# A two-layer streaming-encoder trunk: value passes by token halves at the boundary into the attention, and a reordered first projection

## The chip, the cores and the metric

One core of one Trainium2 chip runs the whole program. The metric is the device time of one execution in microseconds, the median of the runs shown; lower is better. Engines are named as the profile does: PE (TensorE matmul), PEld (its weight loads), DVE (VectorE), ACT (ScalarE), POOL (GpSimd), SP (SyncE, which here issues every DMA).

## The reference

One sequence of 512 tokens with 1024 features passes through two layers. Cut to what matters:

```python
c_act = jax.nn.silu(c)
for i in range(2):
    sh1, sc1, g1, sh2, sc2, g2 = jnp.split(c_act @ w_ada[i] + b_ada[i], 6, axis=-1)
    u = x * (1.0 + sc1) + sh1
    y = gla_mixer(u, ...) if i == 0 else chunk_attention(u, ...)   # both: u @ w_in, mix, @ w_out
    x = layer_norm(ALPHA * x + (1.0 + g1) * y, ln_g[i, 0], ln_b[i, 0])
    u = x * (1.0 + sc2) + sh2
    y = squared_relu_mlp(u, ff_w1[i], ff_w2[i])                    # 1024 -> 4096 -> 1024
    x = layer_norm(ALPHA * x + (1.0 + g2) * y, ln_g[i, 1], ln_b[i, 1])
```

`gla_mixer` is a gated linear attention with 4 heads. `chunk_attention` has 16 heads of 64 features, with a learned bias by distance and a softmax over the keys of the token's own and all earlier chunks.

## The kernel before, in words

Features lie on the 128 partitions, tokens on the free axis; the residual x is eight tiles `xs` of 128 x 512. Every large product is made of three matmuls (`mm3`): each operand is split into a high part (rounded to the matmul's type) and a low part (the rest), and high x high, high x low and low x high are summed in one PSUM bank. So every 128 x 1024 piece of a weight is one "unit": a DMA into a `raw` buffer (5 of them), an ACT copy that makes `whi`, a DVE subtraction that makes `wlo` (POOL for a few units). `wp` holds four such pairs. Some weights that later stages need are split early into `fhi`/`flo`: `f` units stay in SBUF, `c` units are written to DRAM and read back later, already split, by `x` units.

All units stand in one list, `plan`. `next_w` takes the next pair, and `fill(n)` emits units until n pairs are ready. The classes around the engines (`InOrder`, line 39) keep DVE, ACT, POOL and PE instructions in the order in which the code emits them.

The stages, in order of time:

- **First projection** (`gla`, line 622). The 48 modulation vectors of a layer are dot products of `csil` = silu(c), spread over the partitions, with rows of `w_ada`: a DMA of 512 KB and one DVE multiply with a running sum for each (`ada_unit`, line 127). For each of the eight feature tiles k: the multiplies for shift and scale of k, then u[k] = x[k] * scale + shift (high part on ACT, a full copy `uf` and the low part on DVE), the weight unit of k, then 24 matmuls of 512 columns into all eight PSUM banks, 8 high x high, 8 high x low, 8 low x high.
- **GLA**, and its output product, which runs into a `boundary`.
- **`boundary`** (line 328): output product, residual, layer norm and the next u, by two halves of 256 tokens. While the second half is normalised (`stats1`, `stats2`, `ap1`, `ap2`), PE runs the next stage's first four weights (`fg`) on the first half, then on the second, 256 columns at a time.
- **MLP**, in four groups; in layer 0 its units are interleaved with the remaining modulation vectors and with 16 `c` units.
- **Attention** (`att`, line 893). At the second boundary `fg` is q and k of head pairs 0 and 1. Then `vpass` makes the values in two passes of 96 matmuls (tokens stationary, weights moving, 512 columns), into which the scores and the first softmax of heads 0 and 1 are hung. Then a loop over p = 0 to 5: q of pair p+2, scores of head 2p+2 (`s_mm`), k of pair p+2, scores of head 2p+3, the product with the values for heads 2p and 2p+1 (`pv`). DVE, ACT and POOL make the softmax meanwhile (`s_a`: bias and maximum, `s_b1`: subtract, `s_b2`: exponential; `evac_qk`: bias and split of q and k; `fin1` to `fin3`: division).
- The third boundary, the second MLP, the last boundary.

Of the kernel before, what the change touches and what calls it, by code (L numbers as in the profile page):

```python
# [59 lines left out]
def trunk(ctx, tc, xT, c, ada, cols, gk1, gk2, w_qk, w_v, w_g, w_go, a_qk, a_v, a_tab,  # L60
# [47 lines left out]
    nc.sync.dma_start(out=csil, in_=c.to_broadcast([P, D]))  # L108
# [3 lines left out]
    for _ in range(5):  # L112
        T.matmul(warm, one[:, 0:P], one, start=True, stop=True)
    A.activation(out=csil, in_=csil, func=AF.Silu)
# [12 lines left out]
    def ada_unit(l, t, k):  # L127
        raw = rawp.tile([P, D], F32, tag="raw", name=nm("raw"))
        nc.sync.dma_start(out=raw, in_=ada[l, t * 8 + k])
        if (l, t, k) == (0, SH1, 0):  # L130
            nc.sync.dma_start(out=col, in_=cols)
            for ll in range(2):
                for ty in (SC1, G1, SC2, G2):
                    b = C_ADA + ll * 48 + ty * 8
                    G.tensor_scalar(out=col[:, b:b + 8], in0=col[:, b:b + 8], scalar1=1.0, scalar2=None, op0=ALU.add)
            G.tensor_scalar(out=bq8, in0=col[:, C_BQ:C_BQ + 8], scalar1=0.125, scalar2=None, op0=ALU.mult)
            G.tensor_scalar(out=nbgk, in0=col[:, C_BGK:C_BGK + 4], scalar1=-1.0, scalar2=None, op0=ALU.mult)
            G.tensor_scalar(out=gn2, in0=col[:, C_GN:C_GN + 8], scalar1=-0.5, scalar2=None, op0=ALU.mult)
        if t == SC1 and l == 0:
            nc.sync.dma_start(out=xs[k], in_=xT[k * P:(k + 1) * P, :])  # L140
# [28 lines left out]
    def emit_unit():  # L169
# [23 lines left out]
        if state["pos"] == 3:  # L193
            for q in range(2):
                nc.sync.dma_start(out=raw[:, q * S:(q + 1) * S], in_=what[:, q * S:(q + 1) * S])
        else:
            nc.sync.dma_start(out=raw, in_=what)
        hi, lo = split_w(kind in "fF")
        if state["pos"] == 3:
            V.tensor_copy(hi[:, 0:S], raw[:, 0:S])  # L200
            later.append(lambda: A.copy(out=hi[:, S:D], in_=raw[:, S:D]))
            later.append(lambda: lo_of(V, lo, raw, hi))
            ready_w.append((hi, lo))
            return
        if kind == "s":
            for q in range(2):
                A.copy(out=hi[:, q * S:(q + 1) * S], in_=raw[:, q * S:(q + 1) * S])
        else:
            A.copy(out=hi, in_=raw)
# [57 lines left out]
    def add_mlp(l, fgs, ad, keep=()):  # L267
# [60 lines left out]
    def boundary(src, l, gt, open_lnt, mk_cols, fg_evac, events=None, final=False):  # L328
# [262 lines left out]
        fa = [bank(), bank()]  # L591
        n = 3 if late else 2
        fg(0, fa, range(n))
        ap1(0, 3)
        ap2(0, 2)
        stats1(1)
        ap2(0, 3)
        stats2(1)
        fg(0, fa, range(n, 8))
        ap1(1, 0)  # L600
        for p in range(1, 4):
            ap1(1, p)
            ap2(1, p - 1)
        ap2(1, 3)
        fb = [bank(), bank()]
        fg(1, fb, range(8))
        for hf, pf in ((0, fa), (1, fb)):
            fill(1 + hf)
            rest = ()
            for i in range(4):  # L610
                nxt = fg_evac(i, pf[i // 2][:, (i % 2) * HT:(i % 2 + 1) * HT], hf * HT, (hf + 1) * HT)
                for g in rest:
                    g()
                rest = nxt
            for g in rest:
                g()
# [5 lines left out]
    def gla():  # L622
# [9 lines left out]

        u = [act_r() for _ in range(KT)]
        pss = [bank() for _ in range(8)]
        gk_t = wp.tile([P, D], F32R, tag="whi", name="gk_w")
# [5 lines left out]
        G.memset(eps_rms, RMS_EPS)  # L641
        for k in range(KT):
            emit_unit()
            emit_unit()
            if k == 0:
                emit_unit()
            A.activation(out=u[k][:, 0, :], in_=xs[k], func=AF.Identity, scale=mod(0, SC1, k), bias=mod(0, SH1, k))
# [245 lines left out]
    def att(u):  # L893
        es = ExitStack()
# [3 lines left out]
        vt = [ac.tile([P, 8, 192], F32, name=f"vt{i}") for i in range(4)]  # L898
        for i in range(4):
            G.memset(vt[i][:, :, 64:128], 1.0)  # L900
# [68 lines left out]
        def pv(h):  # L969
# [4 lines left out]
            for j in range(4):  # L974
                T.matmul(ps[:, j * P:S], vt[j][:, p, c0:c0 + P], s[j], start=(j == 0), stop=(j == 3))
# [30 lines left out]
        def vpass(n, hooks):  # L1006
            pvb = [bank() for _ in range(4)]
            for j in range(4):
                w = next_w()
                for kk in range(2):  # L1010
                    k = 2 * j + kk
                    for i in range(4):
                        mm3(pvb[i], uk(u, k, i * P, (i + 1) * P), wk(w, kk, S), k == 0, k == KT - 1)
                hooks[j]()
            for i in range(4):
                ov = vt[i][:, n * 4:(n + 1) * 4, :].rearrange("p a (b c) -> p a b c", c=64)[:, :, 0:3:2, :]
                iv = pvb[i].rearrange("p (a b c) -> p a b c", b=2, c=64)
                if i % 2:
                    V.tensor_copy(ov, iv)
                else:  # L1020
                    A.copy(out=ov, in_=iv)

        def both(*fs):
# [207 lines left out]
```

## Time and profile before

| | |
|---|---|
| median of 3 runs | 1232.88 us (1232.21 to 1233.76) |
| the profiled execution | 1231.73 us |
| its span, first to last instruction | 1229.5 us |
| mean granted TensorE clock | 0.991 of full |
| DMA | 192.68 MB, mean 157 GB/s |

| engine | busy us | share of the span |
|---|---|---|
| PE | 1181.4 | 96% |
| PEld | 986.9 | 80% |
| DVE | 834.3 | 68% |
| ACT | 542.9 | 44% |
| POOL | 185.4 | 15% |

A busy PE means that a matmul was in flight. A row of the timeline gives the start, the length from the first instruction's start to the last one's end, and in brackets how long the engine stood idle before it and what ended that. Consecutive matmuls overlap, so the pace of PE is read from start to start.

### The profile page before, as it was taken

The numbers are of one execution on the slowest core, as the hardware profiler recorded it, in microseconds if no ns is written. First come the engines' busy times: TensorE is split into PE (matmuls) and PEld (weight loads), VectorE is DVE, ScalarE is ACT, GpSimd is POOL, SyncE is SP. The second block draws the span as 40 slices with busy tenths as digits, with TensorE's granted clock in tenths as the row PEclk, the third lists the DMA queues.
The fourth block names the chain that finished last, engine by engine and source line by source line (L and its number), as shares of the span: only waits on it lengthen the run. The fifth ranks groups of instructions, "written<-read, shape, count | busy, mean of one in ns | idle before, by whom it ended". The sixth has DMA issues, their size and how long they took to land.

```text
span 1229.5 us, 15417 instructions
## 1 busy us (share of the span) xinstructions
PE 1181.4 (96%) x5834; PEld 986.9 (80%) x5834; DVE 834.3 (68%) x1269; ACT 542.9 (44%) x864; POOL 185.4 (15%) x195
## 2 busy tenths in 40 slices
PE   8999999899999999999999999898999999999995
PEld 5678887788888888888888877668888888888885
DVE  6779579787667676667864788889865443443467
ACT  3265566365243243343483565573642322322324
POOL 2000001620000000004631132226200000000035
PEclk9999999999999999999999999999999999999998
DMA  8846634118878888764025431322165332232201
GB/s 310 280 155 209 230 110 140 50 41 282 284 268 316 280 291 310 261 250 154 2 78 180 146 135 71 128 87 69 35 204 156 92 106 93 88 107 97 89 15 69
DMA packets 57274, 192.68 MB, mean 157 GB/s; under 512 B 6448, under 2 KB 10800, under 8 KB 57200
## 3 DMA queue, kind: packets, MB, share of 16 engines
q1 hardware_dynamic: 57200, 191.70, 45.7%
q8 instruction: 46, 0.75, 0.3%
q14 instruction: 28, 0.23, 0.1%
HBM read 172.80 MB, written 18.87 MB: 156 GB/s over the span
## 4 chain that ended last, share of the span: by engine, by line
PE 58%; DVE 20%; issue 9%; ACT 8%; POOL 3%; DMA 0%; ACTq 0%; DVEq 0%; POOLq 0%
PE ps L47 58%; DVE af L47 5%; ACT af L47 3%; DVE x L47 3%; DVE ar L47 3%; DVE raw L47 2%; DVE wlo L47 2%; ACT ar L47 2%; POOL af L47 1%; POOL x L47 1%; ACT whi L47 1%; DVE u L47 1%; DVE d L47 1%; DVE y L47 1%; ACT e L47 1%
## 5 line engine op out<-in xcount | busy, mean ns | idle before, releaser
L47 PE MATMUL ps<-ar,whi 128*128 128x512 f32 (+1 forms) x2816 | 806.0, 374 | 6.1 <-ACT ar L47 3.3
L47 PEld LDWEIGHTS ps<-ar,whi 128*128 128x128 f32 x2816 | 515.1, 190 | 104.8 <-DVE ar L47 5.3
L47 PE MATMUL ps<-ar,wlo 128*128 128x512 f32 (+1 forms) x1408 | 513.6, 371 | 0.2 <-DVE wlo L47 0.2
L47 PEld LDWEIGHTS ps<-ar,wlo 128*128 128x128 f32 x1408 | 267.0, 190 | 45.7 <-DVE wlo L47 0.8
L47 ACT CAST whi<-raw 128x1024 fp32r<-128x1024 f32 (+1 forms) x171 | 171.4, 1011 | 212.6 <-PE ps L47 187.0
L47 DVE TENSOR_TENSOR wlo<-raw,whi 128x1024 fp32r<-128x1024 f32 x160 | 199.9, 1254 | 33.3 <-ACT whi L47 31.2
L47 DVE SCALAR_TENSOR_TENSOR x<-ps,mods,x 128x512 f32<-128x512 f32 (+1 forms) x96 | 63.0, 658 | 126.4 <-PE ps L47 126.4
L47 POOL TENSOR_TENSOR x<-x,af 128x512 f32<-128x512 f32 x14 | 25.5, 1847 | 805.9 <-ACT af L47 805.9
L47 DVE SCALAR_TENSOR_TENSOR raw<-raw,csil 128x1024 f32<-128x1024 f32 x96 | 115.8, 1218 | 5.9 <-DMA raw<-ada 5.9
L47 DVE TENSOR_TENSOR h<-r 128x512 f32<-128x512 f32 (+1 forms) x72 | 49.2, 688 | 84.0 <-ACT r L47 83.1
L47 PE MATMUL ps<-ar,fhi 128*128 128x256 f32 (+1 forms) x448 | 91.9, 302 | 8.5 <-DVE ar L47 7.6
L47 ACT ACTIVATE r<-ps 128x512 f32<-128x512 f32 (+1 forms) x72 | 39.0, 548 | 130.7 <-PE ps L47 130.5
L47 PEld LDWEIGHTS ps<-ar,fhi 128*128 128x128 f32 x448 | 71.9, 191 | 12.6 <-DVE ar L47 9.0
L47 PE MATMUL ps<-whi,ar 128*128 128x512 f32 x256 | 81.0, 391 | 0.4 <-ACT whi L47 0.4
L47 DVE TENSOR_TENSOR ar<-h,ar 128x512 fp32r<-128x512 f32 (+1 forms) x72 | 45.5, 633 | 39.5 <-ACT ar L47 38.4
L47 PE MATMUL ps<-ar,flo 128*128 128x256 f32 (+1 forms) x224 | 66.9, 298 | 0.0
L47 ACT CAST ar<-h 128x512 fp32r<-128x512 f32 (+1 forms) x72 | 41.2, 573 | 51.8 <-DVE h L47 51.8
L47 PEld LDWEIGHTS ps<-whi,ar 128*128 128x128 f32 x256 | 48.1, 188 | 11.2 <-ACT whi L47 1.3
L47 PE MATMUL ps<-wlo,ar 128*128 128x512 f32 x128 | 50.2, 392 | 1.5 <-DVE wlo L47 1.5
L47 POOL PARTITION_ALL_REDUCE mb<-af x16 | 31.2, 1952 | 125.0 <-DVE af L47 106.7
L47 ACT ACTIVATE af<-x 128x256 f32<-128x256 f32 (+1 forms) x48 | 22.7, 486 | 57.4 <-POOL af L47 31.4
L47 PEld LDWEIGHTS ps<-ar,flo 128*128 128x128 f32 x224 | 42.8, 191 | 1.3
(144 smaller groups left out, 1072.3 us busy)
## 6 DMA issues: line engine op xcount, KB each, us to landing
raw<-f SPq DMA_DIRECT2D x128, 512.0 KB, 4.2
raw<-ada SPq DMA_DIRECT2D x96, 512.0 KB, 4.8
raw<-a_qk SPq DMA_DIRECT2D x16, 512.0 KB, 4.7
khi_q<-fhi SPq DMA_DIRECT2D x12, 512.0 KB, 3.0
klo_q<-flo SPq DMA_DIRECT2D x12, 512.0 KB, 4.4
wlo<-klo_q SPq DMA_DIRECT2D x12, 512.0 KB, 4.2
whi<-khi_q SPq DMA_DIRECT2D x12, 512.0 KB, 3.3
raw<-w_v SPq DMA_DIRECT2D x8, 512.0 KB, 4.5
```

Of the source, the lines that this page charges most:

```text
L47: r = f(*a, **k)
```

## The change

Three things, in the order in which they run.

1. **First projection.** `c` is loaded as one row of 4 KB, spread by two one-row matmuls into PSUM, and silu reads it from there, in place of a broadcast DMA of 512 KB. `ada` rows, x and the weights of three steps are loaded ahead (`head_dma`), the `ada` rows into the pool `act`. `uf` moves from DVE to ACT, the copies of the weight stand ahead of u[k] on ACT, and the multiplies for k+1 are issued within step k (`head_ada`). Eight small POOL additions become one on DVE. After the loop, the first value weight is split ahead of the PSUM evacuations (`fill(1)`), and four of these eight go from ACT to DVE.
2. **MLP of layer 0.** Four value weights take the place of q and k of pairs 0 and 1 as `f` units, and 18 `c` units (q and k of pairs 1 to 7, and four of the output) take the place of 16, two in every five units instead of one in three.
3. **Boundary into the attention.** With `vfill`, both value passes run here by halves of tokens: pass 0 on the first half (part of it ahead of the statistics), pass 1 on the first half, pass 0 and pass 1 on the second. The weights of pass 1 are split here, between the steps of the normalisation (`fill(2)`, `fill(4)`). Then q and k of pair 0 are made in full width, and the attention loop starts at p = -1, for q and k of pair 1 and the first softmax steps of heads 0 and 1, without `pv`. The values stand in two sets of tiles (`vts`).

```diff
+    crow = act.tile([P, D], F32, tag="act", name="crow")[0:1, :]
+    nc.sync.dma_start(out=crow, in_=c)
...
+        T.matmul(cps, one[0:1, 0:P], crow[:, q * S:(q + 1) * S], start=True, stop=True)
+        A.activation(out=csil[:, q * S:(q + 1) * S], in_=cps, func=AF.Silu)
...
+    def head_dma(k):
+        raws = []
+        for t in (SH1, SC1):
+            raws.append(act.tile([P, D], F32, tag="act", name=nm("hraw")))
+            nc.sync.dma_start(out=raws[-1], in_=ada[0, t * 8 + k])
+        if k == 0:
+            nc.sync.dma_start(out=col, in_=cols)
+        nc.sync.dma_start(out=xs[k], in_=xT[k * P:(k + 1) * P, :])
+        raw = rawp.tile([P, D], F32, tag="raw", name=nm("raw"))
...
             if ad:
                 plan.append(("a", ad.pop(0)))
-            if keep and i % 3 == 1:
+            if keep and i % 5 in (1, 3):
                 plan.append(("c", keep.pop(0)))
...
-    kqk = [q + p for p in range(2, 8) for q in (0, 8)]
-    add_mlp(0, [a_qk[0], a_qk[8], a_qk[1], a_qk[9]], ada_list(0, G2) + ada_list(1, SH1, SC1, G1, SC2, SH2),
+    kqk = [q + p for p in range(1, 8) for q in (0, 8)]
+    add_mlp(0, [a_v[k] for k in range(4)], ada_list(0, G2) + ada_list(1, SH1, SC1, G1, SC2, SH2),
...
-    add_units([a_v[k] for k in range(2)], kind="p")
-    add_units([a_v[k] for k in range(2, 8)])
+    add_units([a_v[k] for k in range(4, 8)])
+    add_units([a_qk[0], a_qk[8]])
...
+        if vfill:
+            v_mm, v_out = vfill(un)
+            v_mm(0, fw, 0, range(n))
+            ap1(0, 3)
+            ap2(0, 2)
+            stats1(1)
+            ap2(0, 3)
+            fill(2)
+            stats2(1)
+            v_mm(0, fw, 0, range(n, 8))
+            ap1(1, 0)
+            fill(4)
+            vw = [next_w(False) for _ in range(4)]
+            ap1(1, 1)
+            ap2(1, 0)
+            v_mm(1, vw, 0, range(8))
...
+            v_out(0, 0)
+            v_mm(0, fw, 1, range(8))
+            v_mm(1, vw, 1, range(8))
+            v_out(0, 1)
+            fill(2)
...
         for k in range(KT):
-            emit_unit()
-            emit_unit()
-            if k == 0:
-                emit_unit()
+            if k + 3 < KT:
+                head_dma(k + 3)
...
             A.activation(out=u[k][:, 0, :], in_=xs[k], func=AF.Identity, scale=mod(0, SC1, k), bias=mod(0, SH1, k))
-            uf = gt.tile([P, S], F32, tag="t1", name=nm("uf"))
-            V.tensor_scalar(out=uf, in0=xs[k], scalar1=mod(0, SC1, k), scalar2=mod(0, SH1, k), op0=ALU.mult, op1=ALU.add)
-            w = next_w()
+            A.activation(out=uf, in_=xs[k], func=AF.Identity, scale=mod(0, SC1, k), bias=mod(0, SH1, k))
...
+            if 0 < k < KT - 1:
+                head_ada(k + 1, SH1)
             lo_of(V, u[k][:, 1, :], uf, u[k][:, 0, :])
+            lo_of(V, w[1], raw, w[0])
...
+        fill(1)
         qk = [act_f() for _ in range(4)]
         for h in range(4):
             A.activation(out=qk[h][:, 0, :], in_=pss[h], func=AF.Copy, scale=float(P) ** -0.5)
-            A.copy(out=qk[h][:, 1, :], in_=pss[4 + h])
+            V.tensor_copy(qk[h][:, 1, :], pss[4 + h])
...
+        for is_k in (0, 1):
+            ps = mtile(u, False)
+            if not is_k:
+                v_out(1, 0)
+            else:
+                v_out(1, 1)
+            for f in evac_qk(0, is_k, ps):
+                f()
+            fill(2)
         prev = None
-        for p in range(6):
+        for p in range(-1, 6):
```

How the order moves, at three places. **SP, the first loads.** Before (`raw` from `ada`: the two modulation rows of a step; `col`: the bias columns; `x`, then `raw` from `w_qk`: tile and weight of the step):

```order
L108 DMA csil<-c 128x1024
L129 DMA raw_139<-ada 128x1024
L131 DMA col<-cols 128x196
L129 DMA raw_154<-ada 128x1024
L140 DMA x_88<-xT 128x512
L195 DMA raw_159<-w_qk 128x512 x2
```

and now, `hraw` being the modulation rows:

```order
L109 DMA crow<-c 1x1024
L152 DMA col<-cols 128x196
L153 DMA x_94<-xT 128x512
L157 DMA raw_129<-w_qk 128x512 x2
L150 DMA hraw_123<-ada 128x1024
L150 DMA hraw_125<-ada 128x1024
```

Though the code issues the modulation rows first, the built program has the columns, x and the weight of step 0 ahead of them. **DVE, one step of the first projection** (`ar`: u, low part; `wlo`: the weight's low part; `mods`: the modulation vectors). Before:

```order
L47 SCALAR_TENSOR_TENSOR raw_238,mods<-raw_238,csil 128x1024
L47 SCALAR_TENSOR_TENSOR raw_241,mods<-raw_241,csil 128x1024
L47 TENSOR_TENSOR mods<-mods,col 128x2
L47 TENSOR_SCALAR uf_247<-x_90,mods 128x512
L47 TENSOR_TENSOR wlo_252<-raw_249,whi_251 128x1024
L47 TENSOR_TENSOR ar_119<-uf_247,ar_119 128x512
```

and now, for the same step:

```order
L47 SCALAR_TENSOR_TENSOR hraw_172,mods<-hraw_172,csil 128x1024
L47 TENSOR_TENSOR ar_148<-uf_270,ar_148 128x512
L47 TENSOR_TENSOR wlo_269<-raw_144,whi_268 128x1024
L47 SCALAR_TENSOR_TENSOR hraw_174,mods<-hraw_174,csil 128x1024
L47 TENSOR_TENSOR mods<-mods,col 128x2
```

The two multiplies now belong to the next step and stand around the subtractions of this one; `uf` is gone from DVE. **DVE, the second half of tokens at the boundary into the attention** (`d`, `y`: the statistics; `x`: normalised; `ar`: u, low part), now:

```order
L47 TENSOR_TENSOR wlo_5128<-raw_5125,whi_5127 128x1024
L47 TENSOR_TENSOR wlo_5134<-raw_5131,whi_5133 128x1024
L47 TENSOR_TENSOR d_5137<-y_5119 128x256
L47 TENSOR_TENSOR x_100<-x_100,ps_5103 128x256
L47 SCALAR_TENSOR_TENSOR d_5137<-d_5137,ve_5110 128x256
L47 SCALAR_TENSOR_TENSOR y_5141<-d_5137,y_5119 128x256
L47 TENSOR_TENSOR x_94<-x_94,y_5141 128x256
L47 TENSOR_SCALAR u_5187<-x_95,a_4731,b_4732 128x256
L47 TENSOR_TENSOR wlo_5193<-raw_5190,whi_5192 128x1024
L47 TENSOR_TENSOR wlo_5199<-raw_5196,whi_5198 128x1024
L47 TENSOR_TENSOR x_96<-x_96,y_5141 128x256
L47 TENSOR_SCALAR u_5206<-x_97,a_4731,b_4732 128x256
```

The four rows `wlo` are new there; the other rows stand in the same order as before. On ACT the four copies that make their `whi` stand in the same two gaps.

## Rows read from the trace of the kernel before

**Rows 1.** The page, part 4: the chain that ended last, by engine.
```profile
PE 58%; DVE 20%; issue 9%; ACT 8%; POOL 3%; DMA 0%; ACTq 0%; DVEq 0%; POOLq 0%
```
**Rows 2.** Windows: start:end, length, busy us by engine, PEclk, DMA share, GB/s.
```profile
0.00:62.00 62.00, 55.28 (x204) 39.05 (x205) 40.99 (x70) 20.11 (x31) 9.10 (x28) 0.97 0.85 293
...
300.00:540.00 240.00, 240.00 (x1060) 198.76 (x1059) 164.36 (x221) 84.26 (x101) 0.00 (x0) 1.00 0.82 289
```
**Rows 3.** Timeline of PE, first projection and the matmuls behind it.
```profile
10.96 5.53 PE L47 MATMUL ps<-ar,whi 128*128 128x512 f32 x16 [3.28 <-ACT ar L47]
...
18.14 3.97 PE L47 MATMUL ps<-ar,whi 128*128 128x512 f32 x16
...
26.23 2.11 PE L47 MATMUL ps<-ar,whi 128*128 128x512 f32 x8 [0.27 <-DVE ar L47]
...
30.08 2.11 PE L47 MATMUL ps<-ar,whi 128*128 128x512 f32 x8
...
61.56 3.79 PE L47 MATMUL ps<-ar,gk_w 128*128 128x512 f32 x16
...
66.86 0.50 PE L47 MATMUL ps<-wlo,ar 128*128 128x512 f32 x1 [0.76 <-DVE wlo L47]
```
**Rows 4.** Timeline of DVE, one step of the first projection.
```profile
24.35 1.23 DVE L47 TENSOR_TENSOR wlo<-raw,whi 128x1024 fp32r<-128x1024 f32 x1 [1.33 <-ACT whi L47]
25.49 0.68 DVE L47 TENSOR_TENSOR ar<-uf,ar 128x512 fp32r<-128x512 f32 x1
26.10 1.22 DVE L47 SCALAR_TENSOR_TENSOR raw<-raw,csil 128x1024 f32<-128x1024 f32 x1
```
**Rows 5.** Timeline of DVE, the scale row of step 0.
```profile
8.57 1.23 DVE L47 SCALAR_TENSOR_TENSOR raw<-raw,csil 128x1024 f32<-128x1024 f32 x1 [0.89 <-DMA raw<-ada]
```
**Rows 6.** Windows, two microseconds early in the first projection.
```profile
12.00:14.00 2.00, 2.00 (x6) 1.44 (x5) 2.00 (x3) 0.00 (x0) 1.87 (x5) 0.50 1.04 409
```
**Rows 7.** Timeline of DVE and PE, the GLA stage.
```profile
65.58 1.23 DVE L47 TENSOR_TENSOR wlo<-raw,whi 128x1024 fp32r<-128x1024 f32 x1 [7.23 <-ACT whi L47]
...
117.49 0.73 PE L47 MATMUL ps<-ar,whi 128*128 128x512 f32 x2 [0.67 <-DVE at L47]
```
**Rows 8.** Timeline of PE, boundary into the attention and first value pass.
```profile
601.72 0.40 PE L47 MATMUL ps<-ar,fhi 128*128 128x256 f32 x2
...
605.51 1.28 PE L47 MATMUL ps<-af,ones_c 128*128 128x256 f32 x4 [0.75 <-DVE af L47]
...
617.10 0.38 PE L47 MATMUL ps<-ar,fhi 128*128 128x256 f32 x1 [1.56 <-DVE ar L47]
...
628.59 0.40 PE L47 MATMUL ps<-whi,ar 128*128 128x512 f32 x1
...
641.10 0.50 PE L47 MATMUL ps<-wlo,ar 128*128 128x512 f32 x1 [0.76 <-DVE wlo L47]
```
**Rows 9.** Timeline of PE, MLP of layer 0: one triple of full width.
```profile
340.57 0.61 PE L47 MATMUL ps<-ar,whi 128*128 128x512 f32 x2
...
341.25 0.61 PE L47 MATMUL ps<-ar,whi 128*128 128x512 f32 x2
```
**Rows 10.** Timeline, attention loop: scores, `pv`, k leaves PSUM, its low part.
```profile
706.27 1.45 PE L47 MATMUL ps<-ar,ar 128*128 128x512 f32 x8
...
707.55 4.47 PE L47 MATMUL ps<-af,vt 128*128 128x512 f32 x16
...
708.81 0.69 ACT L47 ACTIVATE f<-ps,col 128x512 f32<-128x512 f32 x1
...
714.28 1.40 DVE L47 TENSOR_TENSOR ar<-f,ar 64x512 fp32r<-64x512 f32 x2
...
728.65 0.69 ACT L47 ACTIVATE f<-ps,col 128x512 f32<-128x512 f32 x1
```
**Rows 11.** Timeline of DVE: one instruction, beside POOL at work and without.
```profile
597.10 0.96 DVE L47 TENSOR_TENSOR x<-x,y 128x256 f32<-128x256 f32 x1
...
617.30 0.41 DVE L47 TENSOR_TENSOR x<-x,y 128x256 f32<-128x256 f32 x1
```

More of the change, by code (lines that the diff above doesn't have):

```diff
@@ L111, in trunk @@
     warm = psp.tile([P, S], F32, tag="ps", name="warm")
-    for _ in range(5):
+    T.matmul(warm, one[:, 0:P], one, start=True, stop=True)
+    for q in range(2):
+        cps = psp.tile([P, S], F32, tag="ps", name=f"cps{q}")
+        T.matmul(cps, one[0:1, 0:P], crow[:, q * S:(q + 1) * S], start=True, stop=True)
+        A.activation(out=csil[:, q * S:(q + 1) * S], in_=cps, func=AF.Silu)
+    for _ in range(4):
         T.matmul(warm, one[:, 0:P], one, start=True, stop=True)
-    A.activation(out=csil, in_=csil, func=AF.Silu)
     tab_ln()
@@ L129, in ada_unit @@
         nc.sync.dma_start(out=raw, in_=ada[l, t * 8 + k])
[L130 to L140, printed above, removed]
         i = t * 8 + k
@@ L192, in emit_unit @@
         raw = rawp.tile([P, D], F32, tag="raw", name=nm("raw"))
[L193 to L197, printed above, removed]
-        hi, lo = split_w(kind in "fF")
[L199 to L209, printed above, removed]
+        nc.sync.dma_start(out=raw, in_=what)
+        hi, lo = split_w(kind in "fF")
+        A.copy(out=hi, in_=raw)
         lo_of(G if kind in "pF" else V, lo, raw, hi)
@@ L631, in gla @@
         at = [gc.tile([P, S], F32, name=f"at{i}") for i in range(2)]
+        for k in range(3):
+            head_dma(k)
         u = [act_r() for _ in range(KT)]
         pss = [bank() for _ in range(8)]
-        gk_t = wp.tile([P, D], F32R, tag="whi", name="gk_w")
+        gk_t = act_r().rearrange("p a b -> p (a b)")
         gk_w = gk_t.rearrange("p (k c) -> p k c", c=P)
@@ L891, in evac_qk, with vfill, v_mm, v_out @@
         return hi, lo
-    def att(u):
-        es = ExitStack()
+    vts, vps = {}, {}
+    def vfill(un):
+        def v_mm(n, ws_, hf, ks):
+            for k in ks:
+                for i in (2 * hf, 2 * hf + 1):
+                    if k == 0:
+                        vps[n, i] = bank()
+                    mm3(vps[n, i], uk(un, k, i * P, (i + 1) * P), wk(ws_[k // 2], k % 2, S), k == 0, k == KT - 1)
+        return v_mm, v_out
+    def v_out(n, hf):
+        for i in (2 * hf, 2 * hf + 1):
+            ov = vts[n][i].rearrange("p a (b c) -> p a b c", c=64)[:, :, 0:3:2, :]
+            iv = vps[n, i].rearrange("p (a b c) -> p a b c", b=2, c=64)
+            if i % 2:
+                V.tensor_copy(ov, iv)
+            else:
+                A.copy(out=ov, in_=iv)
+    def v_tiles(n, pool):
+        vts[n] = [pool.tile([P, 4, 192], F32, name=f"vt{n}_{i}") for i in range(4)]
+        for t in vts[n]:
+            G.memset(t[:, :, 64:128], 1.0)
+    def att(u, es):
         ac = es.enter_context(tc.tile_pool(name="ac", bufs=1))
@@ L897, in att @@
         cur["tmp"] = ab_
-        vt = [ac.tile([P, 8, 192], F32, name=f"vt{i}") for i in range(4)]
-        for i in range(4):
-            G.memset(vt[i][:, :, 64:128], 1.0)
+        v_tiles(1, ac)
         tab_c = ac.tile([P, 16], F32, name="tab_c")
@@ L1004, in fin3 @@
             o.append(r)
[L1006 to L1023, printed above, removed]
-            def f():
-                for x in fs:
-                    x()
-            return f
-        nop = lambda: None
-        s_pre(0)
-        s_pre(1)
-        vpass(0, [nop, nop, lambda: s_mm(0), lambda: s_a(0)])
-        vpass(1, [lambda: s_mm(1), both(lambda: s_b(0), lambda: s_a(1)), nop, nop])
+        for is_k in (0, 1):
+            ps = mtile(u, False)
+            if not is_k:
+                v_out(1, 0)
+            else:
+                v_out(1, 1)
+            for f in evac_qk(0, is_k, ps):
+                f()
+            fill(2)
         prev = None
-        for p in range(6):
+        for p in range(-1, 6):
             pq = mtile(u, False)
```

128 lines of the change are left out of this document (85 added, 43 removed).

## The prediction

> **What bounds the kernel now.** The page's chain comes first: PE holds 58% of it and DVE 20% [rows 1], so PE sets most of the time and DVE parts of it. The windows tell which: in the first 62 us PE is busy 55.28 us, with DMA at 293 GB/s, while in the MLP of layer 0 it is busy for all of 240 us [rows 2]. So time can be won only where PE waits or where it has less to do. I looked for both along PE's timeline. In the first projection a step takes (61.56 - 18.14) / 7 = 6.20 us over the last seven steps, and the second group of eight matmuls waits for the low part of u [rows 3]. There DVE's row shows why: it stands idle 1.33 us for the weight copy, which ACT makes only behind u [rows 4]. At the boundary into the attention PE waits 0.75 us for the statistics, 1.56 us for the second half of u, and 0.76 us for a value weight [rows 8]. The whole sum below is made against the profiled execution, 1231.73 us (span 1229.5); the median of the runs is 1.15 us above it.
>
> **The change, part by part.**
>
> *Start of the first projection: no gain.* The scale row of step 0 landed at 8.57 us [rows 5], behind 512 (c), 512, 98 and 512 KB. By the built order 4, 98, 256, 512, 512 and 512 KB now stand up to it: 260 KB more, at 409 GB/s [rows 6] 0.6 us. So the first matmul moves from 10.96 to 11.6. Step 0 took 18.14 - 10.96 = 7.2 us, part of it at a granted clock of 0.50 [rows 3, 6], 1.2 GHz, the lower of PE's two levels, after 3.28 us of idle. Now the last four warming products end later and the idle is shorter: step 0 takes 5.8 us (three groups at the pace found below) if the clock stays up, 7.2 us if not. Step 1 then starts between 17.4 and 18.8; I take the middle, 18.1, as before, and keep 0.7 us either way.
>
> *Steps 1 to 7: 2.9 us.* Two groups of eight without a wait between them took 30.08 - 26.23 = 3.85 us [rows 3], so three take 5.78 us. With the multiplies a step ahead, the weight copy ahead of u, and `uf` off DVE, DVE has 1.23 + 0.68 + 2 x 1.22 = 4.4 us a step [rows 4] and a small addition, all under PE's 5.78, and it can run ahead by several steps. Gain 7 x (6.20 - 5.78) = 2.9 us. The lower bound is 0 (the loads, see the rivals), the upper the MLP's pace, 0.68 us for three [rows 9] or 5.44 a step: 7 x 0.76 = 5.3 us. I take the pace of the same loop, as the nearest row. The loads need 1.84 MB a step, 318 GB/s, where 409 were reached [rows 6].
>
> *Behind it: 1.4 us.* The first value weight is split ahead of the evacuations, so the 0.76 us wait at 66.86 goes [rows 3]. The evacuations that move to DVE fall where it stood idle 7.23 us [rows 7]; without that cover they would delay `prep` instead. With DVE less late, the wait of 0.67 us at 117.49 [rows 7] goes too. These are at worst kept (0) and can't give more.
>
> *MLP of layer 0: nothing.* Two more `c` units are two ACT copies, two DVE subtractions, two loads and four stores of 512 KB, 3.1 MB. PE has no gap there and DVE has 76 of 240 us free [rows 2].
>
> *Boundary: 4.0 us less, 0.4 back.* From 601.72 to 628.59 the 192 half-width matmuls of q and k take 26.87 us [rows 8], the statistics and all waits within. Without the wait of 1.56, the 0.75 and some 0.9 for the statistics, that is 0.123 us each. The value passes only move. In place of the 192 there are 96 of full width at 0.227 [rows 9]: 21.8 us, and with the statistics and their wait (1.65) 23.4: a gain of 3.4 us. The 1.56 us go because behind the statistics PE now has 36 + 48 value matmuls on the first half, 19 us, where it had 8.6. In that time DVE must do what it did before, plus four subtractions of 1.23 us [rows 4], 4.9 us. The second half is wanted at 606.4 + 19 = 625.5; its first tiles, ready for 617.10 before, would come at 622. Cover 3.5 us. The value weight's 0.76 us goes too (that wait belongs to the old first pass), but q of pair 0 could start with a similar one; its weight can be split once two of the four pairs are free, 5 us ahead, so I count 0.6 of it.
>
> The price is at p = -1. Before, the softmax of heads 0 and 1 ran under 44 us of value matmuls. Now it must run under q and k of pair 1. In the loop the low part of k is done 714.28 + 1.40 - 708.81 = 6.9 us after k leaves PSUM [rows 10], which PE covers with the second scores (1.28), `pv` (4.5) and the next q (5.4). Without `pv` 6.7 us are left, and ACT starts 0.2 us late: PE waits 0.4 us. The bounds are 0 (DVE has no division to do at that p) and 6.4 (a rival).
>
> On the other engines, two subtractions go from POOL to DVE, into the cover just named. The loads of q and k of pair 1 wait for pairs that value matmuls free, 11 us before use, and on SP nothing else stands ahead but a table of 8 KB.
>
> *Sum:* 0 + 2.9 + 1.4 + 0 + 3.4 + 0.6 - 0.4 = 7.9 us. 1231.73 - 7.9 = 1223.8 against the profiled execution; against the median, **1225.0 us**.
>
> One rule would cut this. Half-width matmuls cost 0.123 us and full ones 0.227 in the rows, so two halves cost 0.019 us more than one. The Trainium skill (TensorE: Matmul & The Clock Gate, Back-to-back issue gap) gives columns / 2.4 GHz + 2.5 ns: 109 and 216 ns, a difference of 2.5 ns. By it the 96 pairs save 0.2 us, not 1.8, and the sum is 6.3; the trace decides, and both lie in the range.
>
> **The rivals.**
>
> A. *The first projection doesn't get faster:* the loads, or the ring through DVE, keep the step at 6.2 us. For it: DMA moves 293 GB/s over this stage already [rows 2], the modulation rows now stand behind x and the weight, so the reordering does not do at step 0 what the code says. Against: 409 GB/s [rows 6]. Then 2.9 us stay: 1228.
>
> B. *The second half of u comes late.* An instruction of DVE took 0.96 us beside POOL and 0.41 without [rows 11], and the four subtractions fall beside POOL's normalisation. If each waits 0.8 us and more, and lengthens POOL's work on which the next tile waits, the delay passes the cover of 3.5 us, from which point each us is one on PE. I price it at 3: 1228. The Trainium skill (SBUF — State Buffer, SBUF: two separate sides) says the same as a rule: DVE with two SBUF inputs and POOL hold a shared port by turns, the other "fully blocks". The trace agrees by the rows just named.
>
> C. *The loop's chain, not PE, sets p = -1.* The loop's period is 728.65 - 708.81 = 19.84 us [rows 10], while PE needs 10.9 + 2.6 + 4.5 = 18.0: ACT and DVE set it, and PE lived on a lead. If p = -1 takes that period as well and not 13.5 us, 6.4 us are lost: 1231.4, no change. Against: at p = -1 there is no division and no subtraction for an earlier head.
>
> D. *Slower: the kept pieces outrun DMA in the MLP.* Two `c` units in five instead of one in three raise the stage's 289 GB/s [rows 2] by 1/15 unit of 1.57 MB for each 5.44 us, to 308. If 289 were the ceiling, 233 us of work would take 15 us more, less the 7.9: 1240. It decides as soon as DMA can't pass 300 GB/s there. Against: a share of 0.82 at 289, and 409 elsewhere [rows 6].
>
> **How the numbers follow.** A difference under 0.2%, 2.5 us, can't be told from none. Forecast 0.66 (1221 to 1228.5), A 0.12, B 0.08, C 0.08, D 0.04, and 0.02 for a better pace, below 1221. The low end is the forecast with the MLP's pace in steps 1 to 7 (2.4 us more), the early start (0.7) and no price at p = -1 (0.4), with 1.5 for what a full lead on DVE may remove: 1220. The high end takes in A and B, each with 1 us more: 1229. Outside lie C, D and some mixtures of A with B. Faster than 1230.4: the forecast, A, B and the better pace without their mixtures, 0.84. Within 0.2%: C and mixtures, 0.11. Slower: D and C together with A, 0.05.
>
> **What would show it.** Right: steps of 5.8 us and no wait for `ar` in the first projection, which ends near 58.6; no wait behind the first value matmuls; PE without a gap from the second half's statistics to the scores of head 2, with at most 0.5 us there; the same PE time in the MLP; the period of the attention loop still 19.8. Wrong: waits for `hraw`, `x` or `raw` on DVE or ACT in the steps (A), PE waiting for `ar` at the first matmul of the second half (B), waits in p = -1 and 0 of several us (C), or any PE gap in the MLP with a DMA behind it (D).

## The result, and the profile after

The changed kernel took **1222.22 us** (median of 4 runs, 1222.08 to 1222.72) against 1233.14 for the kernel before beside it: a ratio of 0.9913, 95% interval 0.9896 to 0.993. The forecast was 1225.0 in a range of 1220 to 1229, so the time came 2.8 us under it, and the gain was 10.9 us where the sum had 7.9. The profiled execution took 1222.72 us (span 1220.9).

The page after, busy time by engine and the chain by engine (to [rows 1]):

```profile
PE 1181.6 (97%) x5742; PEld 985.9 (81%) x5742; DVE 831.1 (68%) x1260; ACT 544.8 (45%) x853; POOL 176.6 (14%) x189
...
PE 77%; DVE 13%; ACT 4%; POOL 3%; issue 2%; ACTq 0%; DVEq 0%; POOLq 0%
```

PE's part of the chain grew from 58 to 77%, DVE's fell from 20 to 13. The same two windows as in [rows 2]:

```profile
0.00:62.00 62.00, 60.48 (x230) 44.23 (x231) 43.18 (x72) 30.31 (x45) 5.68 (x20) 1.00 0.82 304
300.00:540.00 240.00, 240.00 (x1060) 198.79 (x1060) 165.50 (x221) 87.62 (x105) 0.00 (x0) 1.00 0.84 298
```

The gain is in the first; in the MLP PE still has no gap, with DMA at 298 GB/s and not 289. The timeline of PE after, the first projection (to [rows 3]), with the warming products ahead of it (`warm`: matmuls on ones, which only keep PE at work until u is there; the profile shows each as two pieces):

```profile
7.21 5.65 PE L47 MATMUL warm<-one 128*128 128x512 f32 x8
12.64 4.25 PE L47 MATMUL ps<-ar,whi 128*128 128x512 f32 x16
...
18.55 3.93 PE L47 MATMUL ps<-ar,whi 128*128 128x512 f32 x16
...
24.13 3.79 PE L47 MATMUL ps<-ar,whi 128*128 128x512 f32 x16
...
56.77 3.79 PE L47 MATMUL ps<-ar,ar 128*128 128x512 f32 x16
...
60.62 0.39 PE L47 MATMUL ps<-wlo,ar 128*128 128x512 f32 x1
```

No row has a wait. Step 1 starts 0.41 us later than before (18.14), steps 1 to 7 take 38.22 us where they took 43.42, and the first low value weight comes 6.24 us earlier (66.86). Further on, PE after, at the statistics of the second half, in the loop, and at the boundary behind the attention:

```profile
598.79 1.28 PE L47 MATMUL ps<-af,ones_c 128*128 128x256 f32 x4 [1.01 <-DVE af L47]
...
734.80 2.42 PE L47 MATMUL ps<-af,vt 128*128 128x512 f32 x8 [0.36 <-ACT af L47]
...
754.67 2.42 PE L47 MATMUL ps<-af,vt 128*128 128x512 f32 x8 [0.43 <-ACT af L47]
...
861.78 0.58 PE L47 MATMUL ps<-ar,fhi 128*128 128x256 f32 x1 [2.34 <-DVE ar L47]
```

and the same places of the kernel before (the first is in [rows 8]):

```profile
745.83 2.42 PE L47 MATMUL ps<-af,vt 128*128 128x512 f32 x8 [0.31 <-ACT af L47]
...
873.14 0.39 PE L47 MATMUL ps<-ar,fhi 128*128 128x256 f32 x1 [2.34 <-DVE ar L47]
```

At the statistics 6.72 us are won (605.51 to 598.79), in the loop 11.03 (745.83 to 734.80), at the last row 11.36 (873.14 to 861.78). Between 598.79 and 734.80 PE never waits. The loop's period is 754.67 - 734.80 = 19.87 us, as before. The spans differ by only 8.6 us because the rest, which is the same program, took 359.12 us after and 356.36 before. Windows there, before and then after:

```profile
860.00:880.00 20.00, 17.52 (x141) 17.02 (x140) 16.76 (x36) 11.94 (x25) 8.53 (x9) 1.00 0.00 1
1200.00:1220.00 20.00, 16.35 (x124) 15.15 (x122) 17.06 (x37) 10.20 (x24) 11.69 (x16) 1.00 0.08 27
```

```profile
860.00:880.00 20.00, 18.22 (x113) 17.53 (x114) 15.07 (x31) 12.83 (x29) 3.63 (x3) 0.83 0.16 53
1200.00:1220.00 20.00, 7.69 (x55) 6.60 (x53) 15.66 (x32) 10.11 (x21) 9.95 (x13) 0.82 0.30 105
```

The granted clock (third figure from the end) dips in these two stretches of this execution after and did not in this one before. The medians, 10.9 us apart, are the better measure.

### The profile page after: what moved, and what is told of

Read it like the earlier page. It is cut to its first block, busy times and chain, and to the rows that moved or that the text cites. A ratio compares the mean times of both kernels' runs of the same rounds, so it can differ in the third digit from the quotient of the medians.

```text
span 1220.9 us, 15202 instructions
## 1 busy us (share of the span) xinstructions
PE 1181.6 (97%) x5742; PEld 985.9 (81%) x5742; DVE 831.1 (68%) x1260; ACT 544.8 (45%) x853; POOL 176.6 (14%) x189
## 4 chain that ended last, share of the span: by engine, by line
PE 77%; DVE 13%; ACT 4%; POOL 3%; issue 2%; ACTq 0%; DVEq 0%; POOLq 0%
PE ps L47 76%; DVE af L47 5%; DVE x L47 3%; ACT af L47 2%; DVE ar L47 2%; POOL af L47 1%; DVE u L47 1%; POOL x L47 1%; DVE wlo L47 1%; PE warm L47 1%; ACT ar L47 1%; DVE d L47 1%; DVE y L47 1%; DVE t L47 0%; DVE raw L47 0%
## 5 line engine op out<-in xcount | busy, mean ns | idle before, releaser
L47 PE MATMUL ps<-ar,whi 128*128 128x512 f32 (+1 forms) x2880 | 822.1, 373 | 0.2 <-DVE ar L47 0.2
L47 PE MATMUL ps<-ar,wlo 128*128 128x512 f32 (+1 forms) x1440 | 526.0, 372 | 0.2 <-DVE wlo L47 0.2
L47 DVE SCALAR_TENSOR_TENSOR raw<-raw,csil 128x1024 f32<-128x1024 f32 x80 | 96.8, 1217 | 0.0
L47 PE MATMUL ps<-ar,fhi 128*128 128x256 f32 (+1 forms) x320 | 70.9, 317 | 6.8 <-DVE ar L47 5.9
L47 PEld LDWEIGHTS ps<-ar,fhi 128*128 128x128 f32 x320 | 53.9, 198 | 10.6 <-DVE ar L47 7.1
L47 PE MATMUL ps<-whi,ar 128*128 128x512 f32 x192 | 60.6, 390 | 0.0
L47 PE MATMUL ps<-ar,flo 128*128 128x256 f32 (+1 forms) x160 | 49.9, 312 | 0.0
L47 PEld LDWEIGHTS ps<-whi,ar 128*128 128x128 f32 x192 | 36.0, 188 | 7.6
L47 ACT CAST fhi<-raw 128x1024 fp32r<-128x1024 f32 x30 | 31.4, 1049 | 23.7 <-DMA raw<-a_qk 12.2
L47 ACT ACTIVATE af<-af 128x1024 f32<-128x1024 f32 (+2 forms) x48 | 32.0, 698 | 20.9 <-DVE af L47 20.4
```

The costliest lines, as they stand in the source:

```text
L47: r = f(*a, **k)
```

## The experiments

**Two halves of the change.** `e1_head` is the kernel before with the change's first projection and the lines behind it; `e2_boundary` has all the rest instead.

> The change's first projection and what stands right behind it alone (broadcast of c by PE, loads ahead of the modulation rows, weight copies ahead of u, low part of u from ACT, multiplies a step ahead, first value weight split early), with the boundary, the attention and the kept pieces of the kernel before. My theory, from the two traces: the statistics at the boundary into the attention come 6.7 us earlier (605.51 to 598.79), so about 1226.4, ratio 0.9946. Rival (what the record says of this part: 2.9 + 1.4 us): 1228.8. Rival (the lead is given back at the old boundary, where a value weight or the second half of u is then late for another reason): 1229 to 1233.

> The rest alone: the first projection of the kernel before, with the change's boundary, attention and kept pieces. My theory: from the statistics of the second half to the attention's loop the trace gains 11.0 - 6.7 = 4.3 us, so about 1228.8, ratio 0.9965, and the two halves add up to the whole change (6.7 + 4.3 = 11.0 of 10.9). Rival (the record's 3.4 + 0.6 - 0.4 us): 1229.5. Rival (the two parts overlap, since the early weights of the head feed the boundary): under 3 us.

Measured: 1226.15 us (ratio 0.9947, 0.9935 to 0.996), 6.7 us less than the 1232.82 of before, as the trace said and not the record's 4.3; and 1230.10 us (0.9978, 0.9969 to 0.9987), 2.7 less, a miss of 1.3. PE of `e1_head` at the statistics, then of `e2_boundary`:

```profile
598.72 1.28 PE L47 MATMUL ps<-af,ones_c 128*128 128x256 f32 x4 [0.79 <-DVE af L47]
```

```profile
606.17 1.28 PE L47 MATMUL ps<-af,ones_c 128*128 128x256 f32 x4 [1.19 <-DVE af L47]
...
742.19 2.42 PE L47 MATMUL ps<-af,vt 128*128 128x512 f32 x8 [0.35 <-ACT af L47]
```

In `e1_head` the lead at the statistics is 605.51 - 598.72 = 6.79 us. The 2.7 us of `e2_boundary` are what the last rival named, but the rows speak against its cause. From the statistics to the loop it takes 136.02 us, the change 136.01 and before 140.32: the boundary's 4.3 us are there, whole, in both. But this execution reached the statistics 0.66 us late, had 3.25 us left at the row that answers to 873.14 (869.89), and its span is 1.4 us shorter: the same last part again. The parts add up to 9.4 of 10.9 us in the medians, and to 6.79 + 4.30 = 11.1 in the rows, where the change has 11.03.

**What set the step of the first projection.** Three edits lie in the step: multiplies a step ahead, weight copies ahead of u on ACT, the f32 copy of u (`uf`) on ACT and not on DVE. A ring is a chain of instructions over several engines that comes back to its start once a step, so that a step can't be shorter than the chain. In the changed kernel DVE turns in 4.76 us:

```profile
28.76 0.69 DVE L47 TENSOR_TENSOR ar<-uf,ar 128x512 fp32r<-128x512 f32 x1 [0.45 <-ACT uf L47]
...
33.52 0.69 DVE L47 TENSOR_TENSOR ar<-uf,ar 128x512 fp32r<-128x512 f32 x1 [0.45 <-ACT uf L47]
```

Before, addition, u and weight copy on ACT, the two subtractions and both multiplies on DVE stood in one ring, which is the 6.20 us of its step. Over these steps (16 to 60 us) DVE and ACT of the kernel before wait for each other only (DVE 9.3 us for weight copies, ACT 31.3 us for the modulation vectors), never for a load. The three runs take edits away and keep the loads three steps ahead:

```diff
 e6_late, in the loop over k (cut):
+            if k: head_ada(k, SH1); head_ada(k, SC1)
-            if 0 < k < KT - 1: head_ada(k + 1, SH1)
-            if k < KT - 1: head_ada(k + 1, SC1)
 e6b_late_uf: the same, and
-            A.activation(out=uf, in_=xs[k], ...)
+            V.tensor_scalar(out=uf, in0=xs[k], ...)
 e45: multiplies ahead as in the change; uf on V, and w_half(0), w_half(1) behind u
```

> The changed kernel, but in the first projection the two modulation multiplies of a step stand at its own start and not a step ahead; the weight copies stay ahead of u on ACT, and the low part of u still comes from ACT. Theory, that a ring through DVE and ACT set the step: two multiplies and the addition 2.7 us, then u and its f32 copy on ACT 1.5, the subtraction 0.6 and the weight's 1.1 on DVE, 5.9 us a step in place of 5.44, so about 3.1 us slower than the changed kernel: 1225.3, with PE waiting for the low part of u. Rival (the loads set the step before, and the change's order of loads freed it): steps stay 5.44, no change. Rival (the multiplies ahead are all of the gain): 6.2 us a step, 1227.5.

> As the last, and the f32 copy of u made by DVE beside ACT's rounded one, as in the kernel before; only the weight copies stay ahead of u. Theory of the ring: two multiplies and the addition 2.7, ACT's u 0.8 (DVE's copy runs beside it), the subtraction 0.6, the weight's 1.1: 5.2 us, under PE's 5.44, so no loss: 1222.2, the same as the changed kernel, and the weight copies moved ahead of u alone give all of the gain of steps 1 to 7. Rival (each of the three edits gives a part): 5.7 to 6.0 us a step, 1224 to 1226.

> The changed kernel with only the multiplies a step ahead left of the three edits in the step of the first projection: the weight copies stand behind u on ACT again, and the f32 copy of u is DVE's again. Theory of the ring: from one addition to the next DVE makes the copy of u 0.5, one multiply 1.2, the subtraction 0.6, the weight's 1.1 (ACT's copy is done 1.9 us after the addition, by then), the other multiply 1.2 and the addition 0.2, 4.9 us in all, under PE's 5.44: no loss, 1222.2. Together with the run that moved only the weight copies this would say that either edit alone takes the ring under PE's pace. Rival (DVE waits for the weight copy again, as its 1.33 us before): over 5.6 us a step and 1223.5 or more.

Measured: 1225.38 us (0.993, 0.9916 to 0.9944), 1221.94 (0.991, 0.9896 to 0.9924) and 1222.27 (0.991, 0.9895 to 0.9925). DVE and PE of `e6_late`, then DVE of `e6b_late_uf`, then of `e45`:

```profile
31.35 0.69 DVE L47 TENSOR_TENSOR ar<-uf,ar 128x512 fp32r<-128x512 f32 x1 [1.59 <-ACT uf L47]
...
37.25 0.69 DVE L47 TENSOR_TENSOR ar<-uf,ar 128x512 fp32r<-128x512 f32 x1 [1.59 <-ACT uf L47]
...
30.66 3.93 PE L47 MATMUL ps<-ar,whi 128*128 128x512 f32 x16 [0.17 <-ACT ar L47]
...
36.56 3.92 PE L47 MATMUL ps<-ar,whi 128*128 128x512 f32 x16 [0.17 <-ACT ar L47]
```

```profile
33.45 0.69 DVE L47 TENSOR_TENSOR ar<-uf,ar 128x512 fp32r<-128x512 f32 x1 [0.30 <-ACT ar L47]
...
38.66 0.69 DVE L47 TENSOR_TENSOR ar<-uf,ar 128x512 fp32r<-128x512 f32 x1 [0.30 <-ACT ar L47]
```

```profile
31.17 0.16 DVE L47 TENSOR_TENSOR mods<-mods,col 128x2 f32<-128x2 f32 x1
...
35.98 0.17 DVE L47 TENSOR_TENSOR mods<-mods,col 128x2 f32<-128x2 f32 x1
```

The rings are 5.90, 5.21 and 4.81 us. Only the first is over PE's 5.44, and it alone sets the step (30.66 to 36.56). So neither edit is needed where the other stands: the multiplies ahead suffice, and so do the weight copies ahead of u. Giving `uf` to ACT is no help: with the multiplies late it costs 3.4 us. No run took both away with the loads still ahead; that the loads alone would have left the step at 6.20 rests on the waits just named.

Note also that PE's row shows a wait of 0.17 us where the step lost 5.90 - 5.44 = 0.46. The bracket does not count what stands around it. In the rows a matmul of 512 columns is in flight for 0.39 us and the next starts 0.23 behind it, an overlap of 0.16 that a wait breaks (drain); and the sixteen behind the wait take 3.93 us and not 3.79, 0.14 more (refill).

**Full width.** `e3_half` makes q and k of pairs 0 and 1 in halves again.

```diff
+    for hf in range(2):
+        for k in range(KT):
+            mm3(ps[:, hf * HT:(hf + 1) * HT], wk(w, k), uk(u, k, hf * HT, (hf + 1) * HT), k == 0, k == KT - 1)
```

> The changed kernel with q and k of pairs 0 and 1 made in halves of 256 columns again, 192 half matmuls in place of 96 of full width; nothing else differs. By the rows (0.123 us for a half, 0.227 for a full one) the 96 pairs cost 96 x 0.019 = 1.8 us, all of it on PE, which has no gap there: 1224.0. By the rule weighed in the record (109 and 216 ns) 96 x 2.5 ns = 0.2 us: 1222.4. In the profile, by the rows each such m-tile takes 5.90 us and not 5.44.

Measured: 1223.24 us (0.9916, 0.9903 to 0.993), 1.0 over the change, though the two kernels' single times overlap; the rows decide. PE, from the first of three such tiles to the scores behind them:

```profile
640.85 0.40 PE L47 MATMUL ps<-ar,whi 128*128 128x256 f32 x2
...
658.12 1.45 PE L47 MATMUL ps<-ar,ar 128*128 128x512 f32 x8
```

17.27 us for 144 halves are 0.120 each, so two halves cost 0.0132 us more than one full matmul, 1.3 us for the 96 pairs. From the statistics (598.91) to the loop (736.22) the run takes 137.31 us, just 1.30 more than the change. The record took 0.0190 from a stretch with waits; their drain and refill were in it. The rule of the Trainium skill weighed there (TensorE: Matmul & The Clock Gate, Back-to-back issue gap) gives 0.0025 for a pair; the run has five times that, so on the difference the measurement decides against both. That section of the Trainium skill gives the rule for a matmul by itself, and about 131 ns for each of a sustained stream of 512 columns, which the record left out. The stream here takes 227 ns for each, so neither figure fits this case.

**What hides the added subtractions.** `e9_dup2` makes each of the four weight subtractions at the boundary three times, `e9_dup1` twice.

```diff
         lo_of(G if kind in "pF" else V, lo, raw, hi)
+        for _ in range(state.get("dup", 0)):
+            lo_of(V, lo, raw, hi)
```

> The changed kernel with each of the four weight subtractions at the boundary into the attention, those that the change adds to DVE ahead of the second half of u, made three times (the same result written again): 8 x 1.23 = 9.8 us more on DVE there, nothing else. Theory of the cover: in the changed kernel the first tiles of the second half are done at 615.5 us and wanted at 618.8, a cover of 3.3 us, and DVE idles 1.15 us for a weight copy in that stretch, which takes up some of it; PE waits 9.8 - 3.3 = 6.5 us less up to 1.15 in front of the second half's first value matmul, and 1227.5 to 1228.7 follow. Rival (the second half of u hangs on POOL or ACT, not on DVE's queue): PE waits under 2 us, 1222 to 1224.

> The changed kernel with each of the four weight subtractions at the boundary made twice: 4.9 us more on DVE. Theory after the run with three: what comes late first is not the second half of u (ready 3.5 us ahead) but the third value weight: in the changed kernel its low part is done at 612.95 us and wanted at 614.0, a cover of 1.0 us, since its copy on ACT waits behind the activations of u, and those behind DVE. With 2.45 us more ahead of it and its own subtraction twice, PE waits about 0.7 us for the copy and 2.0 for the low part: 3 to 3.5 us with the refills, 1225.5. The record's cover (3.5 us at the second half of u) would give 4.9 - 3.5 = 1.4 us or less: 1222.2 to 1223.6.

Measured: 1231.43 us (0.9975, 0.9965 to 0.9985), above the theory, and 1226.87 (0.9941, 0.9928 to 0.9953), 1.4 above it. The timeline of PE and two windows of `e9_dup2`, then PE and one window of `e9_dup1`:

```profile
617.40 0.50 PE L47 MATMUL ps<-whi,ar 128*128 128x512 f32 x1 [1.67 <-ACT whi L47]
...
621.18 0.80 PE L47 MATMUL ps<-wlo,ar 128*128 128x512 f32 x1 [3.28 <-DVE wlo L47]
```

```profile
620.00:625.00 5.00, 3.82 (x9) 3.08 (x10) 4.93 (x5) 0.00 (x0) 0.00 (x0) 0.50 0.32 105
625.00:630.00 5.00, 5.00 (x19) 4.00 (x19) 4.45 (x14) 4.85 (x10) 0.00 (x0) 0.84 0.35 105
```

```profile
614.48 0.50 PE L47 MATMUL ps<-whi,ar 128*128 128x512 f32 x1 [0.64 <-ACT whi L47]
...
617.00 0.50 PE L47 MATMUL ps<-wlo,ar 128*128 128x512 f32 x1 [2.02 <-DVE wlo L47]
```

```profile
615.00:620.00 5.00, 3.00 (x8) 2.40 (x9) 4.93 (x7) 0.66 (x2) 0.00 (x0) 0.77 0.32 105
```

PE waits for the value weights and never for the second half of u. The waits of `e9_dup1` came as told (0.64 and 2.02 for 0.7 and 2.0); the time was missed because behind the waits the granted clock fell, to a mean of 0.77, and in the run with three to 0.50, that is 1.2 GHz, for five microseconds. From the statistics to the loop `e9_dup2` takes 9.6 us more than the change with some 5.8 of idle shown. So the cover that gives out first is not the 3.5 us of u but that of the third value weight. DVE and PE of the changed kernel:

```profile
611.81 2.37 DVE L47 TENSOR_TENSOR wlo<-raw,whi 128x1024 fp32r<-128x1024 f32 x2 [1.15 <-ACT whi L47]
```

```profile
613.78 0.39 PE L47 MATMUL ps<-wlo,ar 128*128 128x512 f32 x1
```

The first of these two subtractions, 1.23 us long, is done at 613.04, and PE wants its result at 613.78 (the 26th of the 48 matmuls from 608.11 on; each weight has twelve): a cover of 0.7 us. The expectation's 1.0 took a matmul one further on.

**The start.** Three runs tried to bring the first matmul forward.

```diff
 e7_order: the loads of the first projection in the order of the code (both modulation rows first)
 e8_order_w2: the same, and
-    for _ in range(4):
+    for _ in range(2):
 e10_full: e7's order, and
-    T.matmul(cps, one[0:1, 0:P], crow[:, q * S:(q + 1) * S], ...)
+    T.matmul(cps, one[:, 0:P], crow[:, q * S:(q + 1) * S], ...)   crow: 128 rows, zeros but for row 0, c by ACT's queue
```

> The changed kernel with the loads of its first projection issued in the order of its code: both modulation rows of step 0 ahead of the bias columns, x and the weight (the build had put them behind). Theory: the first matmul waits for u of step 0, and that for the multiply at 9.00 us, which waits for its row from DMA; csil is there at 7.92 us. With the row there by then the chain is 1.1 us earlier, but the four warming products end only at 12.0 us, so the first matmul comes at 12.1 in place of 12.64, and 0.5 us stay at the end: 1221.7. Rival (all loads in flight share the transfer rate, so that order doesn't matter): the first multiply stays at 9.0 us, no change. Rival (w now lands late): the first matmul later than 12.64, and slower by as much.

> The same, with two warming products in place of four behind the broadcast of c. Theory: the queue of PE is free at 10.6 us, so the first matmul starts with u of step 0 at about 11.5, 1.1 us ahead of the changed kernel: 1221.1, if the granted clock stays at 1.00 over the first step. Rival (the gap of 0.9 us ahead of the first matmul lets the granted clock fall to 0.50 in step 0, as in the kernel before, where step 0 took 7.2 us and not 5.9): step 0 1.3 us longer, and no gain or a small loss against the changed kernel.

> The changed kernel with the modulation rows of step 0 issued first, and c broadcast by a product over all 128 rows (row 0 holds c, the others zeros that POOL writes) in place of a product of one row; c is fetched by ACT's queue. Theory: PE goes from its slow pace (0.85 us a piece of the warming products) to the full one (0.43) after 3.4 to 5.3 us of full products (starts of the kernel before: from 1.50 to 4.94, in one run to 6.77), while the one-row products did not bring it there (rise at 11.4 to 13.2 us, 4.2 to 6.0 us behind them). With full products throughout, the pace rises by 10 us, the warming products end by 11.2, and the first matmul comes with u of step 0 at 11.2 to 11.9 at the full pace: step 1 starts at 17.0 in place of 18.55, and the end comes 1.2 to 1.6 us earlier: 1220.8. Rival (the pace rises at a time that does not hang on what PE does): step 0 waits behind slow warming products as now, no change. Rival (c comes too late for csil through the write of zeros ahead of it): no gain.

Measured: 1221.99 (0.9913, 0.99 to 0.9927), 1222.12 (0.9918, 0.9905 to 0.9932) and 1222.43 us (0.9912, 0.9899 to 0.9926): three misses, none differs from the change. DVE, PE, PE's weight loads and one window of `e7_order`, then PE of `e8_order_w2`, then PE of `e10_full`:

```profile
7.95 1.22 DVE L47 SCALAR_TENSOR_TENSOR hraw<-hraw,csil 128x1024 f32<-128x1024 f32 x1 [6.50 <-ACT csil L47]
...
7.21 6.52 PE L47 MATMUL warm<-one 128*128 128x512 f32 x8
13.17 4.22 PE L47 MATMUL ps<-ar,whi 128*128 128x512 f32 x16
...
11.64 0.34 PEld L47 LDWEIGHTS warm<-one 128*128 128x128 f32 x1 [0.52 <-issue]
12.50 0.34 PEld L47 LDWEIGHTS warm<-one 128*128 128x128 f32 x1 [0.52 <-issue]
...
10.00:14.00 4.00, 4.00 (x8) 1.85 (x7) 2.71 (x7) 2.27 (x4) 0.54 (x3) 1.00 1.03 413
```

```profile
11.97 5.69 PE L47 MATMUL ps<-ar,whi 128*128 128x512 f32 x16 [0.97 <-ACT ar L47]
```

```profile
5.84 3.65 PE L47 MATMUL cps<-crow,one 128*128 128x512 f32 x4 [2.26 <-DMA crow<-c]
9.32 3.60 PE L47 MATMUL warm<-one 128*128 128x512 f32 x8
13.74 4.24 PE L47 MATMUL ps<-ar,whi 128*128 128x512 f32 x16 [0.82 <-ACT ar L47]
```

The order of the loads did its part (the multiply at 7.95 us, not 9.00), but PE's queue was then not free: the eight warming pieces took 6.52 us, 0.85 us apart nearly to the end and not the 0.43 that such pieces reach in other runs. With two products u met PE free at 11.97, but still at the slow pace: its sixteen matmuls took 5.69 us and not 4.25. In `e10_full` the pace had risen by 9.3 us, as expected of full products, but c, loaded by ACT's queue behind the zeros, came 2.3 us late; the third rival took the gain.

**A version ahead of both.** `e11_cdma` gives up the broadcast by PE.

```diff
-    nc.sync.dma_start(out=crow, in_=c)
+    nc.sync.dma_start(out=csil, in_=c.to_broadcast([P, D]))   first of e7's order
-    the two products of one row and their Silu; for _ in range(4):
+    A.activation(out=csil, in_=csil, func=AF.Silu)
+    for _ in range(7):
```

> The changed kernel with c broadcast by the load, as in the kernel before (512 KB), and seven warming products without a break in place of the products of one row; loads of the first projection in the order of the code. Theory: the full pace of PE comes 3.4 to 5.3 us after 1.50 and is kept by the products up to 8.5 to 10.3 us; the broadcast of c by PE, slow and with only one row, is what put csil at 7.92 us and the first matmul behind slow products at 12.6 to 13.2. Here the first matmul comes with u of step 0, as in the kernel before at 10.96, and at the full pace, so that step 1 starts at 16.8 in place of 18.55: about 1220.5, 1.7 us ahead of the changed kernel. Rival (the load of c takes the time back: the row of the scale lands after 9.5 us): the first matmul at 12 or later, no gain. Rival (the gap between the warming products and u lowers the granted clock again): step 0 7.2 us, step 1 at 18.1, 1221.8.

Measured: **1220.38 us** (1220.12 to 1220.89), ratio 0.9892, 0.9877 to 0.9907, beside a before of 1233.94. PE:

```profile
1.50 7.85 PE L47 MATMUL warm<-one 128*128 128x512 f32 x14 [1.50 <-DVE one L47]
10.44 4.08 PE L47 MATMUL ps<-ar,whi 128*128 128x512 f32 x16 [1.09 <-DVE whi L47]
...
16.59 3.96 PE L47 MATMUL ps<-ar,whi 128*128 128x512 f32 x16 [0.26 <-ACT ar L47]
```

Fourteen pieces of the warming products in 7.85 us, most at the full pace, a first matmul at 10.44, and step 1 1.96 us ahead of the change. The lead is still there in the loop (732.73 for 734.80). The interval overlaps the change's; the 1.8 us of the medians and these rows agree. The run changes the broadcast, the warming products and the order of the loads at once; the order alone gave nothing (`e7_order`), the other two were not tried apart.

## Why the prediction was right, step by step

*The right mechanism, one term mis-sized.* What fell short is the step "Two groups of eight without a wait between them took 3.85 us, so three take 5.78" and with it "I take the pace of the same loop, as the nearest row". Those groups were not free of waiting: the first stands right behind one, and the drain and refill of a short wait lie in the spacing of the starts and not in the bracket. In the change a step takes 38.22 / 7 = 5.46 us, in most of them the MLP's pace of 5.44, which the record had as its upper bound: steps 1 to 7 give 5.2 us and not 2.9. That is 2.3 of the 3.1 us by which the rows (11.0) pass the sum (7.9).

*The start: forecast no gain within 0.7.* Step 1 came 0.41 us later, inside the margin, but in part by luck: the first matmul came at 12.64 and not 11.6, and step 0 took 5.9 us, where the forecast was the middle of 5.8 and 7.2. DVE after:

```profile
9.00 1.23 DVE L47 SCALAR_TENSOR_TENSOR hraw<-hraw,csil 128x1024 f32<-128x1024 f32 x1 [7.55 <-DMA hraw<-ada]
...
10.20 1.23 DVE L47 SCALAR_TENSOR_TENSOR hraw<-hraw,csil 128x1024 f32<-128x1024 f32 x1
```

The record moved the scale row alone, by 0.6 us. But both rows now come behind the other loads, so the two multiplies stand one behind the other, and the scale's starts at 10.20 where it was 8.57: 1.63 us, which is the lateness of the first matmul (1.68). Behind that stands the pace of the warming products, as `e7_order` shows.

*Behind it: forecast 1.4, and no more.* The first value pass gave 6.24 - 4.79 (the lead at 56.77 against 61.56) = 1.45 us where the bracket had 0.76, and the wait of 0.67 at 117.49 is gone. By 188.77 the lead is 7.25 (196.02 before), so this part gave 2.5 us: again the brackets counted less than the waits cost. Half a microsecond went back at the waits for the boundary's statistics (0.96 and 1.01 us, 0.65 and 0.75 before), and 6.72 us are left for a forecast of 4.3.

*MLP: forecast nothing, and so it was.* Rival D needed 289 GB/s to be a ceiling; 298 were moved, without a gap on PE.

*Boundary: forecast 3.4 + 0.6 - 0.4 = 3.6, measured 4.3.* Full width gave 1.3 for 1.8. The waits of 1.56 and 0.76 went, and one of 0.18 for a weight copy that the kernel before has just ahead of the latter (639.84); the remaining 0.5 fits the drain and refill at these three, argued and not tried. The price of 0.4 at p = -1 was not charged: no wait stands there, rival C's 6.4 least of all.

*The cover: right that it held, wrong in what it covers.* "Cover 3.5 us" for the second half of u is what the trace after shows (first tiles done at 615.5, wanted at 619.0), but the third value weight had only 0.7, and the prediction did not look at it. What is more than that on DVE there becomes PE's. Rival B's mechanism is visible in small: a pair of subtractions took 2.89 us beside POOL's normalisation (604.40) and 2.37 without (611.81). That fits the shared port of the Trainium skill (SBUF — State Buffer, SBUF: two separate sides), with 0.5 us as its price here; no run took POOL's work away. PE did not feel it.

*Rival A* (steps of 6.2 us) fell with the steps of 5.44.

## What to carry to other kernels

Where PE waits a little in each step of a loop, compare the spacing of its starts with the same loop without waits: here a bracket of 0.27 us stood for 0.76 lost. To find what sets a step, add up the ring of engines from one addition to the next; a step drops to PE's own pace as soon as one edit takes the ring below it, and further edits then give nothing. When a wait is covered, list every operand behind the added work with its own cover, since the tightest may not be the one you watched. At the start of a kernel, look at PE's pace as well as at the loads: here the version that warmed PE with an unbroken run of full products, among other edits, was 1.8 us ahead.

## What the runs showed of the chip

The pace of PE at the start halves its spacing at a time that varies from run to run of the same instructions: a piece of a warming product takes 0.85 us at first and 0.43 later, a factor of two as between 1.2 and 2.4 GHz, while the row of the granted clock reads 1.00 (10 to 14 us of `e7_order`, above). With full products from 1.50 us on, the change came at 4.94 us in the run before, 6.77 in `e2_boundary` and 4.90 in `e11_cdma`. With four single-row pieces between 3.51 and 7.21, it came at 11.41 in the changed kernel, at 13.22 in `e1_head`, whose start is the same, and at about 13.1 in `e7_order`; with full rows in their place (`e10_full`) at 9.33. It was not tried apart from the other edits whether one row or the shorter run of products delays it.

After PE had idled 1.67 and 3.28 us with few matmuls between (`e9_dup2`), the clock was granted at 0.50 from 620 to 625 us; the 9.6 us lost there are 5.8 of waiting, some 2.6 of slow matmuls (from 621.18 to 626.47 twelve of them took 5.3 us, where the changed kernel's pace gives 2.7), and drain and refill.
